# A decoder layer with three token mixers: sums of quarters of X on VectorE, a pair's second product in another PSUM pool, decays in two steps, gates requested a product ahead

## The chip, the cores and the metric

The kernel runs on one core of a Trainium2 chip. The metric is the device time of one execution in microseconds (us); of several runs the median counts. All data are float32.

## The reference

One layer on x of 1024 tokens by 1024 channels. xn is the RMS-normalised x, and one wide projection of xn feeds three mixers and three gates:

```
hn = rms_norm(h, norm_mix_g[l])
proj = jnp.einsum('bsd,de->bse', hn, w_in[l])
za, zb, zc, xbc, dt_raw, g_raw = jnp.split(proj, SPLIT_POINTS, axis=-1)
ya = gmlp_mixer(za, ...); yb = rg_lru_mixer(zb, ...); yc = ssd_mixer(zc, xbc, dt_raw, ...)
gates = jax.nn.sigmoid(g_raw.reshape(bsz, seq, N_BRANCHES, D_MODEL) + b_gate[l])
merged = (gates[:, :, 0] * jnp.einsum('bse,ed->bsd', ya, w_branch_a[l])
          + gates[:, :, 1] * jnp.einsum('bse,ed->bsd', yb, w_branch_b[l])
          + gates[:, :, 2] * jnp.einsum('bse,ed->bsd', yc, w_branch_c[l]))
h = h + jnp.einsum('bsd,de->bse', merged, w_out[l])
hn = rms_norm(h, norm_mlp_g[l])
up = jax.nn.relu(jnp.einsum('bsd,df->bsf', hn, w_mlp_up[l]))
h = h + jnp.einsum('bsf,fd->bsd', up * up, w_mlp_down[l])
```

Mixer A is a gMLP with 128 by 128 position mixing in 8 groups, B a gated linear recurrence, C a Mamba-2 scan with cumulative decays. The result is normalised once more.

## The kernel before, in words

Every float32 operand of a product is split into a high part (rounded to the type that TensorE multiplies in one pass) and a low rest; a product is hi*hi + hi*lo + lo*hi. A cast on ScalarE makes the high part, a subtraction on VectorE (`split`, L132 and L133) or an accumulating DMA on GpSimd the low part.

X, the normalised input, lies in SBUF as 16 tiles: part (high, low) by half of the tokens (`th`) by pair of channel blocks. A quarter of X is a half of the tokens by a half of the channels (`kh`), for two channel blocks at a time (`kp`).

The stages, in order of time. First the rows are normalised and transposed, and V of mixer A is projected. Then 48 products of 48 matmuls each, a queue of units (`one_unit`): weights of 128 columns are loaded on SyncE's queue (`wtile`, L523), cast on ScalarE (L526, L527), finished by an accumulating DMA on GpSimd (L528), and multiplied with X into a PSUM tile of two banks (`product`, L555); two such tiles (`ps`) take turns. Weights are requested two units ahead. After each product its `post` evaluates it, and `step()` lets every pending generator run to its next `yield`; so a `yield` in the code moves work behind the next product. The order on each engine within this stage is set by a scheduler; stretches under `manual_schedule` keep the order of the code.

At the start of this stage `dt_stages` (L592 to 614) makes the cumulative decays of mixer C: two small matmuls into a PSUM tile, `acs` copied out of it, exponentials, `w2`, and then a transpose of `acs` into a third part of the same PSUM tile (L609), copied out, stored in DRAM (L613) and later read back as rows (L664, L670) by the first of the scan's steps.

The last eight units belong to mixer A: gelu (`gelu2`, L235 to L238: ScalarE, VectorE, ScalarE, VectorE) frees the product's PSUM tile, then the mixing matmuls (L859) into `aux` tiles, a multiplication on VectorE (L860) and one on GpSimd (L862), and a store (L863). The group of V that the mixing reads is loaded through GpSimd's queue (L845). Beside these eight units the generator `x_forms` (L878 to 933) prepares sums of quarters of X: T3 of four quarters, and T2, T1, T4, each split into high and low part.

Then come twelve gate pairs (`GatePair`, L935 to 982). They are multiplied in Strassen's manner: seven products (p1 to p7) of 12 matmuls each (`seventh`, L478) with sums of weights (S1 to S4) and the sums of X (T1 to T4) in place of eight. Their PSUM tiles come from two pools of four banks: `aux`, and `gps`, which lies where the `ps` tiles were. Gates are stored in DRAM (L976, L982).

Then the branches: 24 products of the mixers' outputs with w_branch, in the order c, b, a (`branch_unit`). The post loads the gate (L1055) on ScalarE's queue and multiplies it with the product (L1056) on VectorE, which frees the PSUM tile; then it may load and split a tile of the next branch's input (`load_next`, L1040, L132, L133).

The output projection, the second norm and the MLP follow; the change does not touch them.

Of the kernel before, what the change touches and what calls it, by code (L numbers as in the profile page):

```python
# [8 lines left out]
F32 = mybir.dt.float32  # L9
# [27 lines left out]
def trunk_kernel(ctx: ExitStack, tc: tile.TileContext, x, norm_mix_g, w_in, b_gate, gmlp_ln_g, gmlp_ln_b,  # L37
# [554 lines left out]
    def dt_stages():  # L592
        softplus(dt.rearrange("p c h -> p (c h)"), dtr.rearrange("p c h -> p (c h)"))
        tc.keep_in_program_order(actv(na, al, AF.Exp))
        ts(out=adt, in0=dt, scalar1=-1.0, scalar2=None, op0=ALU.mult)
        tt(out=adt, in0=adt, in1=na.unsqueeze(1).to_broadcast([P, NCH, 16]), op=ALU.mult)
        yield
        adt_f = adt.rearrange("p c h -> p (c h)")
        ps_a = aux()
        mm(ps_a[:, :P], tri, adt_f, start=True, stop=True)  # L600
        mm(ps_a[:, P:2 * P], ones, adt_f, start=True, stop=True)
        nc.vector.tensor_copy(out=acs, in_=ps_a[:, :P])
        ts(out=nacs, in0=acs, scalar1=-1.0, scalar2=None, op0=ALU.mult)
        actv(etot, ps_a[:, P:2 * P], AF.Exp)
        w2f = w2.rearrange("p c h -> p (c h)")
        tt(out=w2f, in0=ps_a[:, P:2 * P], in1=acs, op=ALU.subtract)
        actv(w2f, w2f, AF.Exp)
        tt(out=w2f, in0=w2f, in1=dt.rearrange("p c h -> p (c h)"), op=ALU.mult)
        nc.tensor.transpose(out=ps_a[:, 2 * P:3 * P], in_=acs, identity=ident)  # L609
        acsT = act((P, 2, P))  # L610
        nc.vector.tensor_copy(out=acsT[:, 0, :], in_=ps_a[:, 2 * P:3 * P])
        actv(acsT[:, 1, :], ps_a[:, 2 * P:3 * P], AF.Exp)
        nc.gpsimd.dma_start(out=acs_d.rearrange("t r l -> r t l"), in_=acsT)  # L613
        yield

# [231 lines left out]
    def gmlp_unit(g):  # L847
# [17 lines left out]
        def post(ps):  # L865
# [10 lines left out]
    XF.update({n: [[], []] for n in ("T1", "T2", "T4")})  # L876

    def x_forms():  # L878

        def quarter(part, kh, th, kp):  # L880
            return X.tile(part, th, 2 * kh + kp).bitcast(F32)

        def plus(out, in_):
            nc.gpsimd.dma_start(out=out, in_=in_, accum_op=ALU.add)

        def in_halves(name, kp):
            for k in range(2):
                pr = half_((P, 4, P), F32R), half_((P, 4, P), F32R)
                split(pr[0], pr[1], sums[name][kp][:, k])
                for part in range(2):  # L890
                    XF[name][part].append(pr[part])


        first_of = {"T2": (0, 0), "T1": (1, 1), "T4": (1, 0)}
        sums = {n: [act((P, 2, 4, P)) for _ in range(2)] for n in first_of}
        for n, (kh, th) in first_of.items():
            for kp in range(2):
                nc.sync.dma_start(out=sums[n][kp], in_=quarter(0, kh, th, kp))
        t3 = []
        for kp in range(2):  # L900
            d = act((P, 2, 4, P))
            tt(out=d, in0=quarter(0, 1, 1, kp), in1=quarter(0, 0, 1, kp), op=sub)
            tt(out=d, in0=d, in1=quarter(1, 1, 1, kp), op=ALU.add)
            tt(out=d, in0=d, in1=quarter(1, 0, 1, kp), op=sub)
            t3.append(d)
            yield
        for n, (kh, th) in first_of.items():
            for kp in range(2):
                plus(sums[n][kp], quarter(1, kh, th, kp))
        yield  # L910
        for kp in range(2):
            plus(sums["T2"][kp], t3[kp])
        yield
        for kp in range(2):
            in_halves("T2", kp)
            actv(sums["T2"][kp], sums["T2"][kp], AF.Copy, scale=-1.0)
            plus(sums["T1"][kp], sums["T2"][kp])
            plus(sums["T4"][kp], sums["T2"][kp])
        yield
        yield  # L920
        for kp in range(2):
            in_halves("T1", kp)
        yield
        for kp in range(2):
            pr = act((P, 2, 4, P), F32R), act((P, 2, 4, P), F32R)
            split(pr[0], pr[1], sums["T4"][kp])
            for part in range(2):
                XF["T4"][part] += [pr[part][:, k] for k in range(2)]
        sums.clear()
        while queue:  # L930
            yield
        for kp in range(2):
            split(X.tile(0, 1, kp), X.tile(1, 1, kp), t3[kp])

    class GatePair:  # L935
        def __init__(self, br, e):
# [13 lines left out]
            actv(self.o0[:, hsl(0)], self.b1, AF.Copy)  # L950

        def p2(self):
            b0 = aux()
            self.mul(b0, "A12", "B21", True)
            tt(out=self.o0[:, hsl(0)], in0=b0, in1=self.o0[:, hsl(0)], op=ALU.add)

# [89 lines left out]
    def load_next(b, k, fetched=None):  # L1046
# [2 lines left out]
        Y[b].p[0].append(h_)  # L1049
        Y[b].p[1].append(l_)  # L1050

    def branch_unit(b, br, w, e, nxt):
        def post(ps):
            t = act1() if b == "c" and e < 2 else act()
            nc.scalar.dma_start(out=t, in_=gd[br][e])  # L1055
            stt(out=t, in0=t, scalar=1.0, in1=ps, op0=ALU.add, op1=ALU.mult)  # L1056
            if b == "c":
                merged.append(t)
# [581 lines left out]
```

## Time and profile before

| | us |
|---|---|
| median of 3 runs | 2033.15 (2033.07 to 2035.93) |
| profiled execution, whole time | 2034.39 |
| its span, first to last instruction | 2032.6 |
| TensorE busy in the span | 1962.2 |
| VectorE, ScalarE, GpSimd busy | 1200.9, 957.4, 339.0 |
| granted TensorE clock, mean | 0.987 |

The products of the mixers run from about 137 to 790 us, the gate pairs to about 1024, the branches to about 1289. PE is TensorE's matrix multiplication, PEld its loading of weights (which runs beside it), DVE VectorE, ACT ScalarE, POOL GpSimd, SP SyncE; a name with q is the queue that issues DMAs. A timeline row gives start and duration in us, engine, line, operation, tiles written and read, and in square brackets the idle time just before it and what ended that. Tile names stand for what the code calls them: `raw` weights as loaded, `wh` and `wl` their high and low part, `xn` X, `a` and `h` tiles of the activations' pools, `c` and `b` tiles of the branches' inputs.

### The profile page before, as it was taken

Reading aid. Unit: us, or ns where it says so; the run is one execution under the profiler, and the core shown is the slowest. Engines: PE = TensorE matmul, PEld = TensorE weight load, DVE = VectorE, ACT = ScalarE, POOL = GpSimd, SP = SyncE. Lnnn points to the kernel's source line nnn. Section 1 sums busy time; section 2 is a strip of 40 time slices with the busy share of each in tenths; the row PEclk is TensorE's granted clock in tenths of the full one; section 3 lists DMA queues with packets and bytes.
Section 4 is the critical chain, followed back from the end, with each engine's and each line's share of the span. In section 5 each row is a group of like instructions: output and inputs, shape, how many; then the busy total and the mean of one; then the engine's idle time right before and its main releaser. Section 6 shows DMA issues by size and latency. Waiting matters only on the chain.

```text
span 2032.6 us, 23950 instructions
## 1 busy us (share of the span) xinstructions
PE 1962.2 (97%) x9156; PEld 1632.6 (80%) x9156; DVE 1200.9 (59%) x1784; ACT 957.4 (47%) x1387; POOL 339.0 (17%) x422
## 2 busy tenths in 40 slices
PE   8999999999999979999999999999899999999996
PEld 7988878788788767888877888887688887888885
DVE  5584766776767557444342213336765667787787
ACT  6425665757656623444443222246555555253243
POOL 4111222331322444000000220000111111000000
PEclk9999999999999989999999999999999999999998
DMA  4245547366455696333396665521444438634532
GB/s 156 71 144 117 116 104 163 87 132 127 104 119 115 182 229 169 117 114 112 124 331 178 174 149 142 166 83 63 155 147 149 161 136 307 209 129 141 186 106 91
DMA packets 217479, 294.97 MB, mean 145 GB/s; under 512 B 12836, under 2 KB 150260, under 8 KB 217364
## 3 DMA queue, kind: packets, MB, share of 16 engines
q1 hardware_dynamic: 176500, 148.05, 24.1%
q0 software_dynamic: 34928, 123.88, 23.8%
q10 hardware_dynamic: 5936, 21.51, 3.2%
q8 instruction: 72, 1.18, 0.2%
q14 instruction: 43, 0.35, 0.1%
HBM read 178.97 MB, written 67.24 MB: 121 GB/s over the span
## 4 chain that ended last, share of the span: by engine, by line
PE 71%; DVE 12%; DMA 8%; ACT 5%; issue 3%; POOL 1%; SPq 0%; ACTq 0%; POOLq 0%; DVEq 0%
PE aux L478 30%; PE ps L555 27%; PE gps L478 6%; DMA raw<-in_w_in_dram 3%; PE aux L1171 3%; PE aux L257 2%; DVE a L578 1%; DMA wl<-raw 1%; PE aux L815 1%; DVE rsq_q L111 1%; DMA b<-yb_d 1%; DMA raw<-in_w_branch_c_dram 1%; ACT a L1211 1%; DVE a L830 1%; PE aux L734 1%
## 5 line engine op out<-in xcount | busy, mean ns | idle before, releaser
L555 PE MATMUL ps<-xn,wh 128*128 128x512 f32 x1536 | 421.3, 394 | 8.1 <-DVE a L238 8.1
L555 PEld LDWEIGHTS ps<-xn,wh 128*128 128x128 f32 x1536 | 288.6, 189 | 70.2 <-issue 11.0
L555 PE MATMUL ps<-xn,wl 128*128 128x512 f32 x768 | 237.7, 391 | 0.0
L478 PE MATMUL aux<-a,b 128*128 128x512 f32 x864 | 197.3, 389 | 0.0
L526 ACT ACTIVATE wh<-raw 128x1024 fp32r<-128x1024 f32 x72 | 76.1, 1057 | 249.6 <-PE ps L555 201.2
L478 PEld LDWEIGHTS aux<-a,b 128*128 128x128 f32 x864 | 162.2, 188 | 33.7
L555 PEld LDWEIGHTS ps<-xn,wl 128*128 128x128 f32 x768 | 145.3, 189 | 30.7
L478 PE MATMUL aux<-b,wt 128*128 128x512 f32 x672 | 156.9, 389 | 0.0
L478 PEld LDWEIGHTS aux<-b,wt 128*128 128x128 f32 x672 | 126.1, 188 | 26.2
L528 POOL DMA_DIRECT2D wl<-raw x72 | 63.8, 886 | 412.4 <-ACT wl L527 249.8
L478 PE MATMUL aux<-b,b 128*128 128x512 f32 x480 | 110.6, 389 | 0.0
L133 DVE TENSOR_TENSOR wt<-a,wt 128x1024 fp32r<-128x1024 f32 x52 | 65.3, 1256 | 73.5 <-ACT wt L132 73.5
L1056 DVE SCALAR_TENSOR_TENSOR a<-a,ps 128x1024 f32<-128x1024 f32 x22 | 26.8, 1220 | 137.7 <-PE ps L555 124.9
L1392 DVE TENSOR_TENSOR a<-aux,a 128x512 f32<-128x512 f32 x112 | 77.0, 688 | 50.4 <-PE aux L478 50.4
L478 PEld LDWEIGHTS aux<-b,b 128*128 128x128 f32 x480 | 90.1, 188 | 18.7
L133 DVE TENSOR_TENSOR a<-a,a 128x1024 fp32r<-128x1024 f32 (+1 forms) x65 | 65.3, 1013 | 51.3 <-ACT a L132 51.2
L132 ACT ACTIVATE b<-wt 128x1024 fp32r<-128x1024 f32 x60 | 61.8, 1055 | 69.8 <-DMA wt<-u_d 59.7
L555 PE MATMUL ps<-c,wh 128*128 128x512 f32 x320 | 85.5, 389 | 0.0
L578 DVE SCALAR_TENSOR_TENSOR a<-ps,scw,a 128x1023 f32<-128x1023 f32 (+2 forms) x48 | 61.1, 1273 | 39.2 <-ACT a L576 38.5
L478 PE MATMUL aux<-a,wt 128*128 128x512 f32 x336 | 80.3, 396 | 3.4 <-ACT a L1269 3.4
L132 ACT ACTIVATE a<-a 128x1024 fp32r<-128x1024 f32 (+1 forms) x65 | 55.8, 875 | 58.2 <-DVE a L1344 44.4
L478 PEld LDWEIGHTS aux<-a,wt 128*128 128x128 f32 x336 | 64.1, 191 | 17.7 <-ACT a L1269 4.2
(331 smaller groups left out, 3748.8 us busy)
## 6 DMA issues: line engine op xcount, KB each, us to landing
wl<-raw POOLq DMA_DIRECT2D x72, 512.0 KB, 5.2
wt<-u_d SPq DMA_DIRECT2D x54, 512.0 KB
raw<-in_w_in_dram SPq DMA_DIRECT2D x48, 512.0 KB
u_d<-a POOLq DMA_DIRECT2D x48, 512.0 KB, 5.1
g_d<-a POOLq DMA_DIRECT2D x24, 512.0 KB, 2.9
a<-g_d ACTq DMA_DIRECT2D x22, 512.0 KB
rt<-in_w_mlp_up_dram SPq DMA_DIRECT2D x17, 512.0 KB
a<-acs_d POOLq DMA_DIRECT2D x32, 256.0 KB, 8.2
```

What stands on the lines that cost most here:

```text
L111: stt(out=q, in0=r, scalar=nh, in1=r, op0=ALU.mult, op1=ALU.mult)
L132: actv(dst_hi, src, AF.Copy)
L133: (eng or nc.vector).tensor_tensor(out=dst_lo, in0=src, in1=dst_hi.bitcast(F32), op=ALU.subtract)
L257: mm(ps[:, :nt], X.tok(a, k, c), wk[k][w], start=(k == 0 and i == 0), stop=(k == KD - 1 and i == 2))
L478: mm(ps, lhs[l][kk], rhs[r][kk], start=(new and n == 0), stop=(n == 11), skip_group_check=not new)
L526: actv(hi, raw, AF.Copy)
L528: nc.gpsimd.dma_start(out=lo, in_=raw, accum_op=ALU.add)
L555: mm(ps[:, hsl(h)], w[wi][:, k, :], a.rhs(ai, k, h), start=(n == 0), stop=(n == 3 * KD - 1))
L578: stt(out=dst[:, j:], in0=ps[:, :T - j], scalar=taps[3 - j], in1=dst[:, j:], op0=ALU.mult, op1=ALU.add)
L1056: stt(out=t, in0=t, scalar=1.0, in1=ps, op0=ALU.add, op1=ALU.mult)
L1171: mm(ps, M.tok(a, k, c), wo[nb][k][w], start=(k == 0 and a + w == 0), stop=(k == KD - 1 and a == 1))
L1392: tt(out=h, in0=ps, in1=h, op=ALU.add)
```

## The change

Four edits. In `dt_stages` the negated copy `nacs` is no longer made, and the transpose of `acs` goes into a PSUM tile of its own, behind a `yield`. `x_forms` is written anew: before, six quarters were copied by SyncE (L898), and accumulating DMAs of GpSimd (L884, twelve of them) added the others; now all sums are tensor_tensor instructions of VectorE, nine for each `kp`, first all for one `kp` and then for the other. The second product p2 of a pair takes its tile from `gps`, not `aux`. The gates of the branches are requested by `next_gate`, the first ahead of the first branch product and each further one in the post of the product before it.

```diff
@@ dt_stages
-        ts(out=nacs, in0=acs, scalar1=-1.0, scalar2=None, op0=ALU.mult)
...
-        nc.tensor.transpose(out=ps_a[:, 2 * P:3 * P], in_=acs, identity=ident)
+        yield
+        ps_t = aux()
+        nc.tensor.transpose(out=ps_t[:, :P], in_=acs, identity=ident)
         acsT = act((P, 2, P))
-        nc.vector.tensor_copy(out=acsT[:, 0, :], in_=ps_a[:, 2 * P:3 * P])
-        actv(acsT[:, 1, :], ps_a[:, 2 * P:3 * P], AF.Exp)
+        nc.vector.tensor_copy(out=acsT[:, 0, :], in_=ps_t[:, :P])
+        actv(acsT[:, 1, :], ps_t[:, :P], AF.Exp)
@@ x_forms
-        for n, (kh, th) in first_of.items():
-            for kp in range(2):
-                nc.sync.dma_start(out=sums[n][kp], in_=quarter(0, kh, th, kp))
...
-        for n, (kh, th) in first_of.items():
-            for kp in range(2):
-                plus(sums[n][kp], quarter(1, kh, th, kp))
-        yield
-        for kp in range(2):
-            plus(sums["T2"][kp], t3[kp])
-        yield
-        for kp in range(2):
-            in_halves("T2", kp)
-            actv(sums["T2"][kp], sums["T2"][kp], AF.Copy, scale=-1.0)
-            plus(sums["T1"][kp], sums["T2"][kp])
-            plus(sums["T4"][kp], sums["T2"][kp])
...
+        for kp in range(2):
...
+            tt(out=t3, in0=quarter(0, 1, 1), in1=quarter(0, 0, 1), op=sub)
+            tt(out=e, in0=quarter(1, 1, 1), in1=quarter(1, 0, 1), op=sub)
+            tt(out=t3, in0=t3, in1=e, op=ALU.add)
             yield
+            tt(out=d, in0=quarter(0, 0, 0), in1=t3, op=ALU.add)
+            tt(out=d, in0=quarter(1, 0, 0), in1=d, op=ALU.add)
+            in_halves("T2", d)
+            yield
+            tt(out=e, in0=quarter(0, 1, 1), in1=d, op=sub)
+            tt(out=e, in0=quarter(1, 1, 1), in1=e, op=ALU.add)
+            in_halves("T1", e)
+            yield
+            tt(out=d, in0=quarter(0, 1, 0), in1=d, op=sub)
+            tt(out=d, in0=quarter(1, 1, 0), in1=d, op=ALU.add)
...
+            yield
@@ GatePair.p2
-            b0 = aux()
+            b0 = gps.tile([P, HF], F32, tag="gps", name=nm("gps"))
@@ branch_unit
+    def next_gate():
+        if gate_order:
+            b, br, e = gate_order.pop(0)
+            t = act1() if b == "c" and e < 2 else act()
+            nc.scalar.dma_start(out=t, in_=gd[br][e])
+            gates_in.append(t)
...
-            t = act1() if b == "c" and e < 2 else act()
-            nc.scalar.dma_start(out=t, in_=gd[br][e])
+            next_gate()
+            t = gates_in.pop(0)
@@ ahead of the first branch product
+        next_gate()
         one_unit()
```

On TensorE the transpose stood behind 14 of the second product's 48 matmuls; now it stands behind all of them. On SyncE's queue, at the first of the eight last mixer products, stood, in the kernel before (raw: weights of the products; rt: of the gate pairs; a<-xn: the copies):

```order
L523 DMA raw_5902<-in_w_in_dram 128x8x128
L523 DMA raw_5999<-in_w_in_dram 128x8x128
L898 DMA a_5886<-xn_224 128x1024
L898 DMA a_5887<-xn_227 128x1024
L898 DMA a_5888<-xn_552 128x1024
L898 DMA a_5889<-xn_555 128x1024
L898 DMA a_5890<-xn_236 128x1024
L898 DMA a_5891<-xn_239 128x1024
L523 DMA raw_6084<-in_w_in_dram 128x8x128
L523 DMA raw_6165<-in_w_in_dram 128x8x128
L488 DMA rt_6338<-in_w_in_dram 128x8x128
```

and now:

```order
L523 DMA raw_5892<-in_w_in_dram 128x8x128
L523 DMA raw_5995<-in_w_in_dram 128x8x128
L523 DMA raw_6084<-in_w_in_dram 128x8x128
L523 DMA raw_6169<-in_w_in_dram 128x8x128
L488 DMA rt_6336<-in_w_in_dram 128x8x128
```

The six copies are gone, and the weights follow each other. GpSimd's queue likewise loses its twelve accumulates.

On VectorE, from the gelu of the last mixer product to the low half of S1 (wt<-a,wt; L133 is a split, L860 the mixing's multiplication, L502 to L507 the sums of weights), before:

```order
L236 SCALAR_TENSOR_TENSOR a_6392<-a_6392,ps_6342 128x1024
L238 SCALAR_TENSOR_TENSOR a_6391<-a_6392,ps_6342 128x1024
L502 TENSOR_TENSOR a_6417<-a_6339 128x512
L503 TENSOR_TENSOR a_6418<-rt_6338,a_6339 128x512
L506 TENSOR_TENSOR a_6417<-a_6417,rt_6338 128x512
L860 SCALAR_TENSOR_TENSOR a_6423<-aux_6424,vh,bs 128x512
L507 TENSOR_TENSOR a_6418<-rt_6338,a_6417 128x512
L860 SCALAR_TENSOR_TENSOR a_6423<-aux_6430,vh,bs 128x512
L133 TENSOR_TENSOR a_6439<-a_5890,a_6438 128x1024
L133 TENSOR_TENSOR a_6443<-a_5891,a_6442 128x1024
L133 TENSOR_TENSOR wt_6451<-a_6417,wt_6450 128x1024
```

and now:

```order
L236 SCALAR_TENSOR_TENSOR a_6390<-a_6390,ps_6340 128x1024
L133 TENSOR_TENSOR h_6402<-a_6235,h_6401 128x512
L908 TENSOR_TENSOR a_6234<-xn_246,a_6234 128x1024
L238 SCALAR_TENSOR_TENSOR a_6389<-a_6390,ps_6340 128x1024
L502 TENSOR_TENSOR a_6409<-a_6337 128x512
L503 TENSOR_TENSOR a_6410<-rt_6336,a_6337 128x512
L506 TENSOR_TENSOR a_6409<-a_6409,rt_6336 128x512
L861 SCALAR_TENSOR_TENSOR a_6415<-aux_6416,vh,bs 128x512
L507 TENSOR_TENSOR a_6410<-rt_6336,a_6409 128x512
L861 SCALAR_TENSOR_TENSOR a_6415<-aux_6422,vh,bs 128x512
L133 TENSOR_TENSOR a_6433<-a_6234,a_6432 128x1024
L133 TENSOR_TENSOR wt_6437<-a_6409,wt_6436 128x1024
```

A split of T1 and the last add of T4 stand inside the last gelu; ahead of this piece, behind the gelu of the product before, stand five more adds and four splits of the second `kp`.

On VectorE in the branches (L1056, now L1050: gate times product; L133: split of an input tile of branch b or a), from the second product's gate on, before:

```order
L1056 SCALAR_TENSOR_TENSOR c_8161<-c_8161,ps_8112 128x1024
L133 TENSOR_TENSOR b_8357<-b_8357,b_8356 128x1024
L133 TENSOR_TENSOR b_8421<-b_8421,b_8420 128x1024
L133 TENSOR_TENSOR a_8614<-a_8614,a_8613 128x1024
L133 TENSOR_TENSOR b_8485<-b_8485,b_8484 128x1024
L1056 SCALAR_TENSOR_TENSOR a_8225<-a_8225,ps_8176 128x1024
L133 TENSOR_TENSOR b_8549<-b_8549,b_8548 128x1024
L1056 SCALAR_TENSOR_TENSOR a_8289<-a_8289,ps_8240 128x1024
```

and now:

```order
L1050 SCALAR_TENSOR_TENSOR c_8088<-c_8088,ps_8104 128x1024
L133 TENSOR_TENSOR b_8285<-b_8285,b_8284 128x1024
L133 TENSOR_TENSOR b_8349<-b_8349,b_8348 128x1024
L133 TENSOR_TENSOR b_8413<-b_8413,b_8412 128x1024
L1050 SCALAR_TENSOR_TENSOR a_8153<-a_8153,ps_8168 128x1024
L133 TENSOR_TENSOR b_8477<-b_8477,b_8476 128x1024
L133 TENSOR_TENSOR b_8541<-b_8541,b_8540 128x1024
L1050 SCALAR_TENSOR_TENSOR a_8217<-a_8217,ps_8232 128x1024
```

The third product's multiplication stands behind the sixth tile of b now, not the seventh.

More of the change, by code (lines that the diff above doesn't have):

```diff
@@ L935, in trunk_kernel @@
+        assert not queue
+        for kp in range(2):
+            split(X.tile(0, 1, kp), X.tile(1, 1, kp), third[kp])
     class GatePair:
@@ L1050, in load_next @@
         Y[b].p[1].append(l_)
+    gate_order = [(b, br, e) for b, br in (("c", 2), ("b", 1), ("a", 0)) for e in range(KD)]
+    gates_in = []
+    def next_gate():
[4 more added lines that the diff above has]
+            gates_in.append(t)
     def branch_unit(b, br, w, e, nxt):
         def post(ps):
-            t = act1() if b == "c" and e < 2 else act()
-            nc.scalar.dma_start(out=t, in_=gd[br][e])
+            next_gate()
+            t = gates_in.pop(0)
             stt(out=t, in0=t, scalar=1.0, in1=ps, op0=ALU.add, op1=ALU.mult)
```

51 lines of the change are left out of this document (18 added, 33 removed).

## The prediction

> **What bounds the kernel now.** I read the page's table of busy time first, then the waits of TensorE, then its timeline at the waits that the change touches. The table:
>
> ```profile
> span 2032.6 us, 23950 instructions
> PE 1962.2 (97%) x9156; PEld 1632.6 (80%) x9156; DVE 1200.9 (59%) x1784; ACT 957.4 (47%) x1387; POOL 339.0 (17%) x422
> ```
>
> TensorE has 2032.6 - 1962.2 = 70.4 us of idle time, and nothing in the change takes a matmul away. So the change can win only idle time of TensorE, and time in which it ran at a lower clock. The waits of TensorE (line <- what it waited for: total us, times, longest) that lie where the change works:
>
> ```profile
> PE ps L555 <- DVE a L238: 8.1, 2, 8.0
> PE aux L609 <- DVE w L606: 4.2, 1, 4.2
> PE aux L859 <- DMA a<-vn_d: 4.0, 1, 4.0
> PE ps L555 <- DVE a L1056: 1.7, 1, 1.7
> PE aux L478 <- DVE wt L133: 1.5, 2, 1.2
> PE aux L478 <- DVE a L860: 1.0, 1, 1.0
> ```
>
> L609 is the transpose in the decays, L859 and L238 the last mixer products, L478 the gate pairs, L1056 the branch products. The table by stretches (us, then busy us of PE, PEld, DVE, ACT, POOL; granted clock; share of the DMA engines; GB/s) shows what surrounds the waits:
>
> ```profile
> 560.00:690.00 130.00, 128.66 (x640) 105.70 (x640) 89.92 (x124) 81.10 (x115) 37.38 (x46) 1.00 0.54 120
> 706.00:740.00 34.00, 29.93 (x146) 25.09 (x144) 16.01 (x16) 8.45 (x10) 8.72 (x10) 0.93 1.06 262
> 145.00:149.00 4.00, 4.00 (x12) 3.15 (x11) 3.80 (x9) 1.25 (x3) 0.12 (x1) 0.57 0.69 131
> 736.20:740.00 3.80, 3.75 (x16) 3.46 (x16) 0.00 (x0) 1.68 (x3) 0.00 (x0) 0.50 1.05 225
> 748.00:753.00 5.00, 5.00 (x13) 3.95 (x14) 4.47 (x4) 1.27 (x3) 3.82 (x3) 0.54 0.92 300
> ```
>
> Two things: in 706 to 740 the DMA engines are full (1.06, beside 0.54 in the stretch before), and behind each long wait the clock is halved for some four us (0.57, 0.50, 0.54). A removed wait gives that back as well.
>
> **Part B, the sums of quarters (L873 to 933).** The timeline of TensorE through the two waits, and one undisturbed product from the chain:
>
> ```profile
> 189.26 10.91 PE ps L555 x48
> 719.34 1.95 PE L859 MATMUL aux<-wT,a 128*128 128x128 f32 x16
> 736.20 3.76 PE L859 MATMUL aux<-wT,a 128*128 128x128 f32 x16 [4.02 <-DMA a<-vn_d]
> 747.92 2.04 PE L555 MATMUL ps<-xn,wh 128*128 128x512 f32 x4 [7.96 <-DVE a L238]
> 752.92 1.07 PE L555 MATMUL ps<-xn,wh 128*128 128x512 f32 x4
> ```
>
> The waits are 4.02 + 7.96 = 12.0 us. The mixing matmuls of L859 took 3.76 in place of 1.95: 1.8 lost to the clock. From 747.92 to 752.92 stand 12 matmuls; at 10.91/48 = 0.227 each they take 2.7, so 2.3 more is lost. Together 16.1. What caused it:
>
> ```profile
> 697.03 9.10 SPq L898 DMA_DIRECT2D a<-xn  x6
> 706.24 28.32 SPq L523 DMA_DIRECT2D raw<-in_w_in_dram  x2
> 720.81 1.56 POOL L845 DMA_DIRECT2D a<-vn_d  x1
> 738.32 1.06 ACT L526 ACTIVATE wh<-raw 128x1024 fp32r<-128x1024 f32 x1 [25.49 <-DMA raw<-in_w_in_dram]
> 740.75 1.00 ACT L235 ACTIVATE a<-ps 128x1024 f32<-128x1024 f32 x1
> ```
>
> SyncE issues six copies of 512 KB (L898) and only then the next weights, whose data the cast on ScalarE (L526) gets at 738.32. The gelu of a product finished at 719 (L235) stands behind that cast and starts at 740.75, so the PSUM tile stays taken and TensorE waits. GpSimd's L845, the load for the mixing, stands behind six accumulating DMAs and is issued at 720.81. The change drops the 6 copies and 12 accumulates, 9 MB of traffic. The weights are then requested straight behind the ones before, and L845 stands ahead of the next weights' accumulate. I take the whole 16.1 as gone; at the lower bound the waits alone go and the clock loss stays with some other wait (12.0).
>
> What it adds: before, six adds for the two quarters on VectorE and two negations on ScalarE; now eighteen adds. So 12 more, at the row of such an add:
>
> ```profile
> L902 DVE TENSOR_TENSOR a<-xn,xn 128x1024 f32<-128x1024 f32 x2 | 2.4, 1218 | 0.0
> L860 DVE SCALAR_TENSOR_TENSOR a<-aux,vh,bs 128x512 f32<-128x512 f32 x12 | 8.5, 744 | 0.0
> ```
>
> 12 x 1.22 = 14.6 us on VectorE, which idles 34.0 - 16.0 = 18 us in 706 to 740 alone. Between the products the adds are covered: gelu's chain behind a product (L526, L235, L236, L237, L238, all about 1.0 to 1.2) is 5.5 us of a period of 10.9 + 1.7 = 12.6, so VectorE may come 7 us late before a PSUM tile is missed. I cost those at nothing; without that cover each costs its 1.2.
>
> **Part C, where the mixers end and the gate pairs begin (L935 to 960).** Here the cover is thin, since the second quarter's sums now lie in the last two products. From the end of the seventh of the eight mixer products TensorE needs 1.7 + 10.9 + 3.5 (32 mixing matmuls) + 2 x 2.7 (p1, p2) = 21.5 us until p5, whose third matmul needs the low half of S1. VectorE has, in its new order, from that same product's gelu to the low half of S1, 13 rows of full width and 12 of half width: 13 x 1.22 + 12 x 0.74 = 24.7, some 1.5 less for rows that overlap, and 1.0 of ScalarE before the first: 24.2. So p5 waits about 24.2 - 21.5 - 0.5 = 2.2 us, call it 2 to 3. Before, p2 waited 1.0 for an aux tile (L860) and p5 1.2 for S1 (L133). p2 now takes its tile from the pairs' pool, where it waits for the last gelu (L238) alone, which by the same count ends just as p1 does. So the waits come to 2.5 in place of 2.2: 0.3 lost. Does a wait of that size halve the clock?
>
> ```profile
> 1070.85 1.16 PE L555 MATMUL ps<-a,wh 128*128 128x512 f32 x4 [1.72 <-DVE a L1056]
> 1380.30 0.83 PE L1206 MATMUL aux<-ident,a 128*128 128x128 f32 x4 [2.35 <-ACT a L1211]
> 1382.20:1384.00 1.80, 1.80 (x7) 1.41 (x6) 1.74 (x2) 0.97 (x2) 0.00 (x0) 0.50 0.05 9
> ```
>
> After 1.72 the next four matmuls run at full speed (1.16); after 2.35 the clock stood at 0.50. So I add 0.7: C costs 1.0. Bounds: no wait at all, a gain of 2.2; or the rivals' 5 to 6. The Trainium skill, "TensorE: Matmul & The Clock Gate", Part 1, puts the drop to half rate at an idle window of about 3.4 us; by that rule C would cost 0.3 and the time be 0.7 lower. The row of 2.35 speaks against it.
>
> **Part A, the decays (L600 to 613).**
>
> ```profile
> 139.89 0.61 PE L555 MATMUL ps<-xn,wh 128*128 128x512 f32 x2
> 144.74 0.33 PE L609 MATMUL aux<-ident,acs 128*128 128x128 f32 x1 [4.24 <-DVE w L606]
> 148.78 1.09 PE L555 MATMUL ps<-xn,wh 128*128 128x512 f32 x4
> 146.32 1.27 DVE L578 SCALAR_TENSOR_TENSOR a<-ps,scw,a 128x1021 f32<-128x1021 f32 x1
> 149.42 0.74 POOL L613 DMA_DIRECT2D acs_d<-a  x1
> ```
>
> The transpose writes the tile that VectorE still reads for w2 (L606), and 34 matmuls of the second product stand behind it. From 144.82 to 148.78 ten of them took 4.0 in place of 2.3. Now it has a tile of its own and stands behind all 48 matmuls, when acs has long been written: 4.24 + 1.7 = 5.9 gained. What is late next: the second product then ends at about 148.1, and the third needs the first's PSUM tile, free when the last L578 ends at 147.6; half a us to spare, and the removed negation is ahead of it. The store of acs_d and the loads behind it on GpSimd move back by a product, behind one accumulate of weights; nothing of TensorE waits there before. Lower bound: 4.2 without the clock, or nothing (a rival).
>
> **Part D, the gates of the branches.** TensorE's 1.72 at 1070.85 waits for the third product's gate multiplication, and VectorE's rows say why:
>
> ```profile
> 1068.35 1.23 DVE L133 TENSOR_TENSOR b<-b,b 128x1024 fp32r<-128x1024 f32 x1 [5.48 <-ACT b L132]
> 1069.49 1.21 DVE L1056 SCALAR_TENSOR_TENSOR a<-a,ps 128x1024 f32<-128x1024 f32 x1
> ```
>
> The multiplication stands behind the split of the seventh tile of b, which had come late. In the new order it stands behind the sixth, requested before it. So the wait goes: 1.7. Bounds: 1.7 gained, or as much lost, since one more gate of 512 KB is loaded early, on ScalarE's queue ahead of a cast, among the loads that are late there.
>
> **Sum.** -16.1 (B) + 1.0 (C) - 5.9 (A) - 1.7 (D) = -22.7. The profiled execution took 2034.39 us, 1.8 of it around its span of 2032.6; it would come to 2011.7. The median of the runs, 2033.15, lies 1.2 below it: 2033.15 - 22.7 = 2010.4.
>
> **Rivals.**
>
> GpSimd and VectorE in each other's way at the pairs (0.15):
>
> ```profile
> 777.20 2.41 POOL L862 TENSOR_TENSOR a<-a,a 128x1024 f32<-128x1024 f32 x1 [10.97 <-DVE a L860]
> 795.68 5.50 POOL L862 TENSOR_TENSOR a<-a,a 128x1024 f32<-128x1024 f32 x1 [9.55 <-ACT a L132]
> 802.79 2.80 DVE L133 TENSOR_TENSOR wt<-a,wt 128x1024 fp32r<-128x1024 f32 x1 [1.06 <-ACT wt L132]
> ```
>
> One multiplication on GpSimd took 5.50 where another took 2.41, and the split on VectorE beside one took 2.80, not 1.22. With more adds there, S1 comes 1.6 later and S3 behind that multiplication 3.1: 4.7 and 1 of clock, so 2016. The Trainium skill, "SBUF — State Buffer", "Who interferes with whom", says the same of any VectorE instruction with two SBUF inputs beside a GpSimd one that reads SBUF: one blocks the other. That speaks against the change.
>
> ScalarE held by a sum (0.10): the casts of T2 and T1 stand in its order ahead of L526 and L235. If a sum comes over 7 us behind a product's end, TensorE waits for L238 again: say 4 and 2 of clock, 2016.4. Against it: by the same rows the first T2 sum ends before the next product does.
>
> The decays do not gain (0.05): the third product waits in the transpose's place. 2010.4 + 5.9 = 2016.3.
>
> Slower (0.03): the late weights come of other traffic, not of the copies. Then B stays, and the 12 adds, in order before gelu, add up to 14.6: -5.9 - 1.7 + 14.6 = +7, 2040. It decides if the weights requested at 706 still land behind 732, the product's end. The share of 1.06 beside 0.54 speaks against it.
>
> **How the numbers follow.** The forecast holds 0.67. The range: below, C without waits (-3.2) and the runs' spread of about 1.5, 2005.7; above, the three rivals at 2016 and that spread, 2018. It leaves out little beyond the slower case. A measurement of this kernel tells about 0.2%, 4.1 us, from no change: all cases but the slower one lie beyond it; faster 0.95, same 0.02, slower 0.03.
>
> **What would show it.** Right: no wait of TensorE in the second product and none over 1 us between the mixer products; DMA share near 0.5 to 0.7 at 700 to 735; S1's low half as the longest wait of the first pair, 2 to 3 us; no wait for L1050 near the fourth branch product. Wrong: an L235 of ScalarE that starts over 5 us after its product, or the pairs' first 5 products taking over 20 us.

## The result, and the profile after

| | before | after |
|---|---|---|
| median of 4 runs, us | 2034.48 (2033.07 to 2035.93) | 2013.74 (2012.43 to 2014.22) |
| profiled execution, us | 2034.39 | 2012.43 |

The ratio of after to before is 0.9897, 95% interval 0.988 to 0.9914: faster by 1.0%. The forecast was 2010.4, with 2005.7 to 2018.0 as its range.

The head of the page of the changed kernel (busy us, share, count):

```profile
span 2010.6 us, 23918 instructions
PE 1957.1 (97%) x9156; PEld 1629.6 (81%) x9156; DVE 1215.9 (60%) x1795; ACT 955.3 (48%) x1385; POOL 327.3 (16%) x410
```

VectorE has 15.0 us more work than before (1215.9 - 1200.9), GpSimd and ScalarE have less. The span is 22.0 us shorter. To see where, take the start of the same five instructions on TensorE in both timelines: the first matmul of the decays (L600), the first mixing matmuls of the last eight mixer products (L859, now L860), p1 and p4 of the first gate pair (L478), and the first and last rows of the branch products (L555). Before:

```profile
136.67 0.38 PE L600 MATMUL aux<-adt,tri 128*128 128x128 f32 x2
693.11 1.95 PE L859 MATMUL aux<-wT,a 128*128 128x128 f32 x16
790.33 2.98 PE L478 MATMUL gps<-xn,wt 128*128 128x512 f32 x12
813.51 2.93 PE L478 MATMUL gps<-a,a 128*128 128x512 f32 x12
1025.28 1.21 PE L555 MATMUL ps<-a,wh 128*128 128x512 f32 x4 [0.78 <-ACT a L944]
1288.12 0.62 PE L555 MATMUL ps<-c,wl 128*128 128x512 f32 x2
```

After:

```profile
136.79 0.38 PE L600 MATMUL aux<-adt,tri 128*128 128x128 f32 x2
686.95 1.95 PE L860 MATMUL aux<-wT,a 128*128 128x128 f32 x16
767.39 2.98 PE L478 MATMUL gps<-xn,wt 128*128 128x512 f32 x12
793.50 2.90 PE L478 MATMUL gps<-a,a 128*128 128x512 f32 x12
1005.24 1.21 PE L555 MATMUL ps<-a,wh 128*128 128x512 f32 x4 [0.78 <-ACT a L928]
1266.32 0.61 PE L555 MATMUL ps<-c,wl 128*128 128x512 f32 x2
```

The differences of neighbouring starts are the stretches (the branches up to the end of their last row):

| stretch | before | after | change | forecast |
|---|---|---|---|---|
| A: decays and most mixer products | 556.44 | 550.16 | -6.28 | -5.9 |
| B: the last mixer products, up to p1 | 97.22 | 80.44 | -16.78 | -16.1 |
| C: p1 to p4 of the first pair | 23.18 | 26.11 | +2.93 | +1.0 |
| the other gate pairs | 211.77 | 211.74 | 0.0 | 0 |
| D: branches | 263.46 | 261.69 | -1.77 | -1.7 |

What is left of the 22.0, 0.1, lies ahead of L600 and behind the branches. All four terms have the sign that was forecast, and C is the one that was mis-sized. Its place in the timeline of TensorE:

```profile
772.45 4.58 PE L478 MATMUL gps<-xn,wt 128*128 128x512 f32 x12 [2.08 <-DVE a L238]
776.87 0.63 PE L478 MATMUL aux<-h,wt 128*128 128x512 f32 x2
778.36 2.58 PE L478 MATMUL aux<-h,wt 128*128 128x512 f32 x10 [0.86 <-DVE wt L133]
781.25 3.02 PE L478 MATMUL gps<-h,wt 128*128 128x512 f32 x12 [0.31 <-ACT a L934]
785.64 2.58 PE L478 MATMUL aux<-xn,wt 128*128 128x512 f32 x10 [0.92 <-DVE wt L133]
```

The first row is p2: it waits 2.08 us for the last gelu (L238) and then takes 4.58 us, where p1 took 2.98. The table by stretches (us; busy us of PE, PEld, DVE, ACT, POOL; granted clock; share of the DMA engines; GB/s) shows the clock there, and the full DMA engines of before gone:

```profile
703.00:736.00 33.00, 33.00 (x163) 27.94 (x162) 30.32 (x29) 14.85 (x17) 12.98 (x12) 1.00 0.67 164
764.00:767.30 3.30, 3.30 (x32) 3.30 (x31) 3.30 (x5) 2.06 (x3) 0.03 (x1) 1.00 0.40 159
772.40:777.00 4.60, 4.55 (x13) 3.64 (x14) 4.60 (x7) 1.58 (x2) 0.87 (x1) 0.63 0.51 125
```

### The profile page after: what moved, and what is told of

It reads as the page before. It is cut to its first block, busy times and chain, and to the rows that moved or that the text cites. A ratio compares the mean times of both kernels' runs of the same rounds, so it can differ in the third digit from the quotient of the medians.

```text
span 2010.6 us, 23918 instructions
## 1 busy us (share of the span) xinstructions
PE 1957.1 (97%) x9156; PEld 1629.6 (81%) x9156; DVE 1215.9 (60%) x1795; ACT 955.3 (48%) x1385; POOL 327.3 (16%) x410
## 3 DMA queue, kind: packets, MB, share of 16 engines
q0 software_dynamic: 33200, 117.59, 22.5%
## 4 chain that ended last, share of the span: by engine, by line
PE 83%; DVE 11%; ACT 4%; issue 2%; POOL 1%; ACTq 0%; DVEq 0%; POOLq 0%
PE ps L555 34%; PE aux L478 29%; PE gps L478 8%; PE aux L257 4%; PE aux L1166 3%; PE aux L816 1%; PE aux L735 1%; PE aux L731 1%; DVE a L578 1%; ACT a L1206 1%; DVE a L831 1%; DVE h L752 1%; DVE rsq_q L111 1%; DVE a L702 0%; DVE a L133 0%
## 5 line engine op out<-in xcount | busy, mean ns | idle before, releaser
L555 PE MATMUL ps<-xn,wh 128*128 128x512 f32 x1536 | 418.3, 392 | 0.0
L555 PEld LDWEIGHTS ps<-xn,wh 128*128 128x128 f32 x1536 | 286.8, 188 | 61.2 <-issue 2.8
L555 PE MATMUL ps<-xn,wl 128*128 128x512 f32 x768 | 236.6, 389 | 0.0
L478 PE MATMUL aux<-a,b 128*128 128x512 f32 x864 | 197.3, 389 | 0.0
L478 PEld LDWEIGHTS aux<-a,b 128*128 128x128 f32 x864 | 162.2, 188 | 33.7
L526 ACT ACTIVATE wh<-raw 128x1024 fp32r<-128x1024 f32 x72 | 76.1, 1057 | 214.7 <-PE ps L555 203.7
L555 PEld LDWEIGHTS ps<-xn,wl 128*128 128x128 f32 x768 | 144.2, 188 | 30.2
L478 PE MATMUL aux<-b,wt 128*128 128x512 f32 x672 | 156.9, 389 | 0.0
L478 PEld LDWEIGHTS aux<-b,wt 128*128 128x128 f32 x672 | 126.2, 188 | 26.1
L478 PE MATMUL aux<-b,b 128*128 128x512 f32 x480 | 110.6, 389 | 0.0
L133 DVE TENSOR_TENSOR wt<-a,wt 128x1024 fp32r<-128x1024 f32 x52 | 63.7, 1226 | 72.3 <-ACT wt L132 72.3
L478 PE MATMUL gps<-xn,wt 128*128 128x512 f32 x432 | 103.8, 394 | 2.1 <-DVE a L238 2.1
L1050 DVE SCALAR_TENSOR_TENSOR a<-a,ps 128x1024 f32<-128x1024 f32 x22 | 26.8, 1220 | 130.2 <-PE ps L555 117.4
L478 PEld LDWEIGHTS aux<-b,b 128*128 128x128 f32 x480 | 90.1, 188 | 18.7
L478 PEld LDWEIGHTS gps<-xn,wt 128*128 128x128 f32 x432 | 82.1, 190 | 19.6 <-issue 2.5
L133 DVE TENSOR_TENSOR a<-a,a 128x1024 fp32r<-128x1024 f32 (+1 forms) x65 | 66.7, 1033 | 49.1 <-ACT a L132 49.1
L132 ACT ACTIVATE b<-wt 128x1024 fp32r<-128x1024 f32 x60 | 61.9, 1053 | 69.7 <-DMA wt<-u_d 63.8
L555 PE MATMUL ps<-c,wh 128*128 128x512 f32 x320 | 85.5, 389 | 0.0
L478 PE MATMUL aux<-a,wt 128*128 128x512 f32 x336 | 80.0, 395 | 3.3 <-ACT a L1264 3.3
L132 ACT ACTIVATE a<-a 128x1024 fp32r<-128x1024 f32 (+1 forms) x65 | 55.8, 874 | 55.7 <-DVE a L1339 44.4
```

What stands on the lines that cost most here:

```text
L132: actv(dst_hi, src, AF.Copy)
L133: (eng or nc.vector).tensor_tensor(out=dst_lo, in0=src, in1=dst_hi.bitcast(F32), op=ALU.subtract)
L478: mm(ps, lhs[l][kk], rhs[r][kk], start=(new and n == 0), stop=(n == 11), skip_group_check=not new)
L526: actv(hi, raw, AF.Copy)
L555: mm(ps[:, hsl(h)], w[wi][:, k, :], a.rhs(ai, k, h), start=(n == 0), stop=(n == 3 * KD - 1))
```

## The experiments

Twelve kernels were run. The table gives the stretches of each, taken from its timeline at the same instructions, and its median with the ratio to the kernel before on the same chip (95% interval). The letters are those of the table above.

| run | A | B | C | D | median, us | ratio |
|---|---|---|---|---|---|---|
| before | 556.44 | 97.22 | 23.18 | 263.46 | | |
| after | 550.16 | 80.44 | 26.11 | 261.69 | 2013.74 | 0.9897 (0.988 to 0.9914) |
| a_alone | 551.52 | 96.68 | 23.17 | 263.48 | 2029.29 | 0.9973 (0.9964 to 0.9982) |
| b_alone | 556.22 | 80.43 | 26.79 | 263.58 | 2021.54 | 0.9932 (0.9916 to 0.9949) |
| copies_kept | 550.09 | 80.43 | 23.94 | 261.82 | 2013.33 | 0.9893 (0.9878 to 0.9909) |
| copies_dve | 555.24 | 85.82 | 23.21 | 263.31 | 2024.68 | 0.995 (0.9935 to 0.9965) |
| six_acc | 556.71 | 81.97 | 23.20 | 265.53 | 2019.79 | 0.9922 (0.9907 to 0.9937) |
| weights_first | 556.62 | 98.99 | 23.18 | 263.31 | 2035.26 | 1.0001 (0.9992 to 1.0011) |
| p2_aux | 550.12 | 80.44 | 26.10 | 261.77 | 2013.94 | 0.9894 (0.9879 to 0.9909) |
| no_gates | 550.16 | 80.43 | 26.09 | 263.65 | 2014.94, a single run | |
| no_mul5 | 550.15 | 80.43 | 23.88 | 261.98 | 2011.42 | 0.9884 (0.9852 to 0.9917) |
| early_sums | 550.13 | 80.44 | 20.75 | 261.70 | 2008.60 | 0.987 (0.9853 to 0.9886) |
| early_aux | 550.12 | 80.43 | 20.75 | 263.32 | 2009.40, a single run | |
| early_mul | 550.14 | 80.43 | 19.53 | 261.96 | 2006.66 | 0.9859 (0.9844 to 0.9874) |

### The parts by themselves

**a_alone**: the kernel before with the new `dt_stages`.

> The kernel before with the new decays alone. Theory: the wait of 4.24 us for L606 and the slow matmuls behind it go, nothing takes their place; about 6 to 6.7 us less than the kernel before, 2028, and no wait of TensorE between 137 and 165 us. Rival: the third product waits for its PSUM tile in the transpose's place; then 2034, with a wait for L578 near 148 us.

The transpose stands behind 48 matmuls and waits for nothing; nor do the matmuls behind it:

```profile
150.73 0.27 PE L610 MATMUL aux<-ident,acs 128*128 128x128 f32 x1
150.76 1.18 PE L555 MATMUL ps<-xn,wh 128*128 128x512 f32 x4
```

A falls by 4.9 in this run and by 6.3 in the changed kernel; two small waits elsewhere in the mixers (0.8 and 0.4 us) make a good part of the difference. In the medians this run is 5.6 us below the kernel before on its chip, a little under the 6 to 6.7 expected. The decays' part is worth 4.9 to 6.3 us, and nothing took the transpose's place.

**b_alone**: the kernel before with the new `x_forms`.

> The kernel before with the new sums alone (old decays, p2 in the mixers' aux pool, gates as before). By the two profiles the stretch of the last mixer products gained 16.4 us and the boundary to the pairs lost 2.5. Theory of separate terms: 2034.9 - 16.4 + 2.5 to 4 (p2 in aux waits for the multiplication L861 behind the last gelu, 1 to 2 us longer than for the gelu): 2021 to 2022.5. Rival: the parts help each other (the decays' earlier order decides when weights are requested); then the wait for L238 is back in part and the time is 2026 or more.

B is 80.43, as in the changed kernel, without the new decays, and the median lies in the range expected; the parts add up and do not need each other.

**p2_aux**: the changed kernel with

```
-            b0 = gps.tile([P, HF], F32, tag="gps", name=nm("gps"))
+            b0 = aux()
```

> The changed kernel with p2's tile from the mixers' aux pool, as before. Theory: p2 waits for the first multiplication L861 of the seventh unit (it ends 2.5 us behind the last gelu) in place of the gelu: its wait grows from 2.1 to 4.4 us, the wait of 0.9 for S1 goes: 1.0 to 1.5 us more than the changed kernel, 2015. Rival: the pool makes no difference, 2013.7, with the same wait of p2.

p2's wait grew as forecast, and yet the first pair took as long (C 26.10 beside 26.11), since p5, p6 and p3 then waited for nothing:

```profile
775.64 5.08 PE L478 MATMUL aux<-xn,wt 128*128 128x512 f32 x12 [4.46 <-DVE a L861]
780.57 2.92 PE L478 MATMUL aux<-h,wt 128*128 128x512 f32 x12
783.33 2.88 PE L478 MATMUL gps<-h,wt 128*128 128x512 f32 x12
786.04 2.98 PE L478 MATMUL aux<-xn,wt 128*128 128x512 f32 x12
```

VectorE is busy without a gap there and decides when the pair gets on; the pool only decides at which product TensorE waits. The edit of the pool is worth nothing in the changed kernel.

**no_gates**: the changed kernel with `next_gate` taken out again.

> The changed kernel with the gates of the branches requested as before, in the post of their own product. Theory: the wait of 1.7 us for the third product's gate multiplication near the fourth branch product is back, since it stands behind the split of the seventh tile of b again; span 2010.6 + 1.7 = 2012.3 within what runs differ. Rival: with the pairs ending 21 us earlier the tiles of b come in time and no wait shows; then the requests ahead were worth nothing.

The wait is back, at the same product and for the same multiplication (L1040 in this kernel), and D is 263.65 in place of 261.69:

```profile
1051.26 1.16 PE L555 MATMUL ps<-a,wh 128*128 128x512 f32 x4 [1.98 <-DVE a L1040]
```

### What held up the last mixer products

**copies_kept**: the changed kernel, whose sums again start from six copies made by SyncE:

```
+        for n, (kh, th) in (("T2", (0, 0)), ("T1", (1, 1)), ("T4", (1, 0))):
+            for kp in range(2):
+                nc.sync.dma_start(out=sums[n][kp], in_=X.tile(0, th, 2 * kh + kp).bitcast(F32))
```

> The changed kernel with the six SyncE copies of quarters put back (the adds start from the copied tiles, so there are as many adds; no accumulating DMA). Theory: the copies on SyncE's queue made the next weights late, and the accumulates on GpSimd's queue made the load for the mixing late. Then the long wait for L238 (8 us and 2.3 of clock) comes back and the wait of the mixing matmuls for vn_d does not: 2013.7 + 10 = 2024. Rival: the accumulates caused both waits; then 2014. Rival: only the sum of both kinds of traffic filled the DMA engines; then a wait of 0 to 3 us and 2014 to 2018.

B is 80.43: without accumulates the copies cost nothing. The theory that the copies ahead of the weights on SyncE's queue made the wait by themselves has fallen.

**copies_dve**: the kernel before with

```
-                nc.sync.dma_start(out=sums[n][kp], in_=quarter(0, kh, th, kp))
+                nc.vector.tensor_copy(out=sums[n][kp], in_=quarter(0, kh, th, kp))
```

> The kernel before with the six copies of quarters made by VectorE in place of SyncE; the twelve accumulates stay. Theory (copies make the weights late, accumulates the load for the mixing): the wait of the mixing matmuls (4.0 and 1.8 of clock) stays, the wait for L238 goes: 2034.5 - 10.3 = 2024. Rival: the accumulates caused both waits; then 2034. Rival: only both kinds of traffic together are too much; then both waits go, 2018 to 2020.

The size came near the theory's, 10.2 us less in the medians, but by another way. The wait for vn_d, which should have stayed, is gone (its load L845 is issued at 710.30, not 720.81), and 4.9 us of waits for the gelu stay. ScalarE's rows say why:

```profile
727.24 0.63 ACT L132 ACTIVATE h<-a 128x512 fp32r<-128x512 f32 x1 [14.67 <-DMA a<-a]
727.78 1.04 ACT L526 ACTIVATE wh<-raw 128x1024 fp32r<-128x1024 f32 x1
729.82 1.01 ACT L235 ACTIVATE a<-ps 128x1024 f32<-128x1024 f32 x1
```

ScalarE waits 14.67 us for the sum T2 that the seventh of the twelve accumulates makes; the cast of the weights and the gelu stand behind its split. This is the step that the rival "ScalarE held by a sum" feared of the new kernel; it is found in this variant of the kernel before.

**six_acc**: the kernel before with

```
-                nc.sync.dma_start(out=sums[n][kp], in_=quarter(0, kh, th, kp))
+                tt(out=sums[n][kp], in0=quarter(0, kh, th, kp), in1=quarter(1, kh, th, kp), op=ALU.add)
...
-                plus(sums[n][kp], quarter(1, kh, th, kp))
```

> The kernel before with the six copies and the first six of the twelve accumulating DMAs replaced by six adds on VectorE; the other six accumulates, on which the splits wait, stay. The run with all twelve and no copies won 10 of the 16 us, the run with copies and no accumulates all of it. Theory now: an accumulate keeps the 16 DMA engines busy for about 2.6 us (31 us for twelve by the shares of the queue), and the weights are late when these add up. Then six fewer free 16 us of the engines, the weights are in time and the wait for L238 falls under 1 us: 2034.9 - 16 = 2019. Rival: not the amount but the chain decides (ScalarE's casts stand behind splits of sums that the last accumulates make, and L526 and gelu behind those); then 3 to 5 us of wait for L238 stay and the time is 2023 to 2025.

1.2 us of wait is left and B is 81.97, 1.5 above the changed kernel's: half the accumulates do nearly no harm. ScalarE still stands before the split of T2, but for less long:

```profile
720.72 0.63 ACT L132 ACTIVATE h<-a 128x512 fp32r<-128x512 f32 x1 [6.31 <-DMA a<-a]
```

The first accumulate for T2 was issued at 714.75, which is 5.4 us later than in copies_dve (709.33), and the split starts 6.5 us earlier (720.72 beside 727.24). So the number of accumulates ahead of it decides when T2 is there, and the chain that the rival names is the way by which that reaches the gelu.

**weights_first**: the kernel before with the weights requested earlier:

```
+        ahead(AHEAD + 3)
         for n, (kh, th) in first_of.items():
             for kp in range(2):
                 nc.sync.dma_start(out=sums[n][kp], in_=quarter(0, kh, th, kp))
```

> The kernel before, all copies and accumulates kept; only the order on SyncE's queue differs: the third weights are requested behind the first copy, not behind the sixth. By the trace of before, that request is issued at 706.24 and its data moves from 716 on beside accumulates, 50 packets of 512 bytes a microsecond beside as many of 4 KB, and lands 32 us after its issue. Theory now: the two queues take turns packet by packet, so small packets starve once accumulates run; asked for ahead of five copies, the weights land before that, ScalarE's cast L526 is done before 725 and the wait for L238 shrinks to the 3 to 5 us that the late sum of T2 leaves, as in the run without copies: 2024 to 2027. Rival: the amount of traffic decides, whatever the order; then L526 still starts at 735 or later and the time stays at 2034.

No gain (B 98.99). This time no weights were missing; ScalarE stood before the split of T2 for 21 us, and L526 and the gelu behind it:

```profile
739.69 0.63 ACT L132 ACTIVATE h<-a 128x512 fp32r<-128x512 f32 x1 [21.46 <-DMA a<-a]
740.22 1.04 ACT L526 ACTIVATE wh<-raw 128x1024 fp32r<-128x1024 f32 x1
742.48 3.75 PE L859 MATMUL aux<-wT,a 128*128 128x128 f32 x16 [8.44 <-DMA a<-vn_d]
```

TensorE's longest wait there, the last row, is for vn_d: its load stands behind the accumulates too and was issued at 728.93. Behind it come waits for the gelu of 2.12 and 2.29 us. So earlier weights alone gain nothing, and the rival (the traffic, in whatever order) stands. The two rows of the DMA queues in the pages (packets, MB, share of 16 engines) price the traffic, first before, then after; q0 is GpSimd's queue, q1 SyncE's:

```profile
q1 hardware_dynamic: 176500, 148.05, 24.1%
q0 software_dynamic: 34928, 123.88, 23.8%
```

```profile
q1 hardware_dynamic: 175636, 144.91, 24.1%
q0 software_dynamic: 33200, 117.59, 22.5%
```

On q0, 23.8% of 2032.6 less 22.5% of 2010.6 is 31.4 us of all 16 engines, 2.6 for each of the twelve accumulates; on q1 the same sum gives 5.3, 0.9 for each copy (both within 2 us, since the shares are rounded to 0.1%). In B the price is not a sum of the two, though: six copies cost 0, twelve accumulates 5.4 (85.82 - 80.44), both together 16.8. (The 5.4 may be low: the profiled execution of copies_dve is the fastest of its four, 2.6 us below their median, and the clock stayed full behind its longest wait.) GpSimd's rows in the kernel before show the link:

```profile
706.54 0.88 POOL L884 DMA_DIRECT2D a<-xn  x1 [2.50 <-DMA a<-xn]
719.69 0.86 POOL L884 DMA_DIRECT2D a<-xn  x1 [3.02 <-DMA a<-xn]
721.73 2.40 POOL L884 DMA_DIRECT2D a<-a  x2
```

Each of the first six accumulates waits in GpSimd's queue for its copy to land, the last till 719.69, and only then come the accumulates that make T2, at 721.73. Without the copies (copies_dve) the first six were issued from 702.30 to 709, and the two for T2 at 709.33 and 719.70:

```profile
709.33 0.85 POOL L884 DMA_DIRECT2D a<-a  x1 [0.39 <-DVE a L904]
719.70 0.85 POOL L884 DMA_DIRECT2D a<-a  x1 [5.97 <-DVE a L904]
```

In the kernel before, the weights (at 738.32) and T2 came late together. weights_first shows that T2 alone is enough to make the gelu late; whether the weights alone would be was not tried.

### What the first gate pair waits for

**early_sums**: the changed kernel without the `yield` behind T3 of each `kp`:

```
             tt(out=t3, in0=t3, in1=e, op=ALU.add)
-            yield
             tt(out=d, in0=quarter(0, 0, 0), in1=t3, op=ALU.add)
```

> The changed kernel without the two yields behind T3, so that each later sum is made a product earlier and the second quarter's are all done ahead of the last gelu. Theory: p2 waits 2.08 us for the last gelu (and runs its 12 matmuls 1.6 us slower than p1) because sums and splits stand ahead of that gelu on VectorE; then p2 waits for nothing, p5 at most 1 us, and the time is 3 to 4.5 us below the changed kernel, about 2010. Rival: GpSimd's multiplications hold VectorE there; then the waits move to p5 and p3 and at most 1 us is won.

C falls from 26.11 to 20.75, more than was expected, and the median from 2013.74 to 2008.60. Of the waits of the first pair only p3's is left:

```profile
770.01 5.70 PE L478 MATMUL gps<-xn,wt 128*128 128x512 f32 x24
775.55 3.27 PE L478 MATMUL aux<-h,wt 128*128 128x512 f32 x12
782.92 2.56 PE L478 MATMUL aux<-xn,wt 128*128 128x512 f32 x10 [0.93 <-DVE wt L133]
```

**no_mul5**: the changed kernel with

```
-            nc.gpsimd.tensor_tensor(out=y, in0=y, in1=u2, op=ALU.mult)
+            if g != 5:
+                nc.gpsimd.tensor_tensor(out=y, in0=y, in1=u2, op=ALU.mult)
```

> The changed kernel without one of GpSimd's eight multiplications (L863 of the sixth of the eight last mixer products; that block of mixer A is stored without its factor u). Beside that multiplication a split of VectorE took 2.88 us, in place of 0.68. Theory: without it the split takes 0.7, the last gelu ends 2.2 us earlier and p2 waits for nothing; p5 then waits some 2.6 for S1, since VectorE's chain decides all along; the first pair takes 23.5 to 25.5 us from p1 to p4 in place of 26.1. Rival: the split is long for another reason (its inputs come from ScalarE late); then it takes 2.9 again and p2 waits 2.1.

It was aimed at these rows of the changed kernel:

```profile
759.91 3.23 POOL L863 TENSOR_TENSOR a<-a,a 128x1024 f32<-128x1024 f32 x1 [6.71 <-DVE a L861]
760.81 2.88 DVE L133 TENSOR_TENSOR h<-a,h 128x512 fp32r<-128x512 f32 x1
```

Without GpSimd's instruction the same split took 0.68, and all that follows came 2.2 earlier; p2 waits for nothing and p5 2.4 us for S1:

```profile
761.22 0.68 DVE L133 TENSOR_TENSOR h<-a,h 128x512 fp32r<-128x512 f32 x1
773.48 0.70 PE L478 MATMUL aux<-h,wt 128*128 128x512 f32 x2
776.56 4.14 PE L478 MATMUL aux<-h,wt 128*128 128x512 f32 x10 [2.38 <-DVE wt L133]
```

C is 23.88, which is 2.2 less than in the changed kernel.

**early_mul**: early_sums with the last two multiplications on VectorE:

```
-            nc.gpsimd.tensor_tensor(out=y, in0=y, in1=u2, op=ALU.mult)
+            (nc.vector if g >= 6 else nc.gpsimd).tensor_tensor(out=y, in0=y, in1=u2, op=ALU.mult)
```

> The variant with the sums a product earlier, and the last two units' multiplications (L863) on VectorE in place of GpSimd. In that variant p3 still waits 0.9 us for S4's split. Theory of the port (GpSimd's multiplications hold VectorE's splits: rows of 2.1 and 2.9 us in place of 1.2 and 0.7 beside them): the two cost VectorE 2 x 1.2 and give back 3.1, so p3's wait goes, 0 to 1 us less than that variant, 2008. Rival: VectorE's added work delays S1 and S4 by 1.2 to 2.4; then p5 and p3 wait 1 to 2 us longer, 2010.

C is 19.53, 1.2 less than in early_sums where 0 to 1 was expected, and no product of the first pair waits. Its median, 2006.66, is the lowest of all, and the interval of its ratio (0.9844 to 0.9874) lies below that of the change (0.988 to 0.9914).

**early_aux**: early_sums with p2's tile from `aux`.

> The variant with the sums a product earlier, and p2's tile from aux again. There VectorE is no longer behind at the boundary (p2 waits for nothing). Theory: now the pool decides: p2 waits for the first multiplication behind the last gelu as it did in the kernel before, 1 us, and the first pair takes 1 to 2 us longer than the variant's 20.75 from p1 to p4. Rival: the wait is given back by S4's, and the first pair takes the same time.

p2 waits 0.88 us and p3 no longer does; C is 20.75 in both. The rival held: here, too, the pool moves a wait and is worth nothing in the pair. This single run shows something else, though. D is 263.32, as without the gates requested ahead, for a wait of the sixth branch product:

```profile
1056.42 1.16 PE L555 MATMUL ps<-a,wh 128*128 128x512 f32 x4 [1.62 <-DVE a L1049]
```

The multiplication of the fourth product stands behind the splits of two tiles of b, and the first of these came later: ScalarE waited 10.14 us for it, and 8.60 in the changed kernel. There the same multiplication (1058.57, 1.21 long) ended 0.15 us before the sixth product's first matmul (1059.93), so part D had nothing to spare. What delayed the tile is not shown.

## Why the prediction was right, and where not

- **What bounds the kernel** (idle time and half-clock time of TensorE): right. The stretches that were to gain, gained by their waits and the clock behind them.
- **Part B, size**: right, 16.8 beside 16.1; VectorE's 12 added adds cost nothing between the products, as said.
- **Part B, cause**: right for the load of the mixing, which stands behind the accumulates: issued at 710.30 (copies_dve) it made no wait, at 720.81 (before) 4.0, at 728.93 (weights_first) 8.4. For the gelu, the step that failed is "SyncE issues six copies of 512 KB (L898) and only then the next weights". Copies alone cost nothing (copies_kept), and weights requested ahead of five of them gain nothing (weights_first). No wait comes without the accumulating DMAs: 2.6 us of all DMA engines each, with the split of T2, and so the gelu, waiting for one that stands behind six others. Alone they cost 5.4 of the 16.8; the other 11.4 come only together with the copies, which hold the accumulates back. The sum came out right because the change drops both, which as to the cause is luck. What the row of 738.32 named, DMA raw, was late in that execution, and not alone.
- **The rival "Slower"** (0.03), late weights from other traffic than the copies, had the cause more nearly than the forecast; but that traffic was mostly the accumulates, which the change drops as well. In the changed kernel the cast L526 starts at 712.92 and had waited for TensorE, not for weights.
- **Part C**: mis-sized, 2.9 in place of 1.0. The step that failed is "13 x 1.22 + 12 x 0.74": it counted every split at the duration that it has alone. One took 2.2 us longer beside GpSimd's multiplication. Without that multiplication (no_mul5) the pair waits as forecast, p5 for S1 and 2.4 us (2 to 3 said), and C is 0.7 above before (1.0 said). That this is so close is partly luck: the clock behind that wait cost 1.6, not 0.7, and the waits of p6 and p3 that the kernel before has (0.32 and 0.31), which the sum left out, went.
- **The rival of GpSimd and VectorE** (0.15) thus came true in part: named rightly as a mechanism, but put at the multiplications beside S1 and S3, where 1.2 of it reaches TensorE (C of early_sums less C of early_mul; both have the sums a product earlier). The larger part struck a unit earlier. The Trainium skill, "SBUF — State Buffer", "Who interferes with whom", states that a VectorE instruction with two SBUF inputs and a GpSimd one that reads SBUF block each other; 2.88 beside 0.68 agrees.
- **Part A**: right, 6.3 beside 5.9, and the third product had its tile in time.
- **Part D**: right, 1.8 beside 1.7, for the reason given (no_gates). It was near to failing all the same: the next multiplication had nothing to spare, and in early_aux it made a wait of 1.62.
- **p2's pool**: that p2 waits for the last gelu is what the trace shows, but that the gelu "ends just as p1 does" was 2.1 us off, because of that split. The edit itself is worth nothing.
- **The signs**: one that was named as a sign of being wrong came, "the pairs' first 5 products taking over 20 us": 20.8 (767.39 to 788.22), and 17.9 in the kernel before. It is the loss of part C. S1's low half was not the pair's longest wait (0.86; p2's was 2.08). Between the mixer products four waits of 1.1 us for a cast (L132) stay, which the kernel before has too; the rest came as named.
- **From the sum to the median**: the profiled execution was forecast at 2011.7 and took 2012.43. The median was put 1.2 below the profile, as it had been before; here it lies 1.3 above it. With the 0.7 that makes the 3.3 between 2010.4 and 2013.74. The 0.7 is small because errors cancel: A, B and D gained 1.1 more than forecast, C lost 1.9 more.

## What to carry to other kernels

A wait is put down to what came last; before pricing its removal, look for what else was late at that time, since a fix of one of two late inputs gains nothing, and a fix of what delays both gains all. An accumulating DMA is cheap to issue and dear to run: where a vector engine idles, an add there costs less than the traffic. At a boundary, count the rows of the engine that has no gap, with the durations they have beside their neighbours, not alone; which buffer a product waits for hardly matters there. Count the half-clock time behind a wait as a chance, not as a part of its price: like waits had it and had it not.

## What the hardware showed

- Two DMA queues shared the engines packet by packet. In 728 to 732 of the kernel before, with weights in packets of 512 bytes on q1 and accumulates of 4 KB on q0, both moved 202 packets (columns: packets, MB, share of 16 engines):

```profile
q0 software_dynamic: 202, 0.76, 94.8%
q1 hardware_dynamic: 202, 0.10, 12.6%
```

  In each 2 us from 716 to 732 the two counts agree within 5. So 512 KB of weights at 0.10 MB in 4 us need some 20 us (an estimate from these rows), while in copies_kept 0.70 MB of q1 moved in 4 us (710 to 714). The Trainium skill, "DMA: Bandwidth & Descriptors", "Queues, rings and completion order", says that an engine takes its queues in turn by packets; the equal counts agree.
- TensorE's clock can fall behind a wait as short as 2.08 us (p2: granted clock 0.63 over the next 4.6 us), but the length of a wait does not tell whether it falls. After 1.72 us, and 1.98 in no_gates, the next matmuls ran at full speed; so they did after 3.47 us in copies_dve (granted clock 1.00 from 737.2 to 745). The same 24 matmuls of the MLP behind the same wait took 7.36 us in the kernel before and 5.74 in copies_kept:

```profile
737.18 1.17 PE L555 MATMUL ps<-xn,wh 128*128 128x512 f32 x4 [3.47 <-DVE a L238]
1450.98 7.36 PE L478 MATMUL aux<-a,wt 128*128 128x512 f32 x24 [2.58 <-ACT a L1269]
1427.05 5.74 PE L478 MATMUL aux<-a,wt 128*128 128x512 f32 x24 [2.59 <-ACT a L1269]
```

  So the prediction's step from "after 2.35 the clock stood at 0.50" to a cost for a wait of 2.5 was a guess that one execution bears out and another need not. The Trainium skill, "TensorE: Matmul & The Clock Gate", Part 1, gives an idle window of about 3.4 us that runs freely; the drops after 2.08 and 2.35 us speak against its length, and that like waits end differently agrees with its running freely.
- The blocking between VectorE and GpSimd goes either way. In copies_kept, whose adds stand in a slightly different order, the same multiplication of GpSimd took 7.93 us and the split beside it 0.68; C is 23.94 there, as without the multiplication.
